# Feed-forward weights split at higher priority, the set-up moved behind a gate evacuation, the first weights in four pieces

## The chip, the cores and the metric
The kernel runs on one core of one Trainium2 chip. The metric is the device time of the whole program in microseconds (us); lower is better. A core has five engines with a queue each that runs in order: TensorE (PE, matmuls; its weight loads are PEld), VectorE (DVE), ScalarE (ACT), GpSimd (POOL) and SyncE (SP, which here only issues DMAs).

## What is computed
Two layers of a first block, each of them a gated feed-forward, an attention mixer and a second feed-forward, then two layers of a second block, each of them a hybrid attention and a feed-forward. There are 256 tokens of width 1024, all in fp32. The six feed-forward stages are what the change touches:

```python
def swiglu(x, w_gate, w_up, w_down):
    return (jax.nn.silu(x @ w_gate) * (x @ w_up)) @ w_down
# first block, per layer (D_FF = 2816):
x = x + 0.5 * swiglu(rms_norm(x, norm_ffn1[l]), w_ffn1_gate[l], w_ffn1_up[l], w_ffn1_down[l])
x = x + hybrid_mixer(rms_norm(x, norm_mix[l]), ...)
x = x + 0.5 * swiglu(rms_norm(x, norm_ffn2[l]), w_ffn2_gate[l], w_ffn2_up[l], w_ffn2_down[l])
# second block, per layer:
gate, up = jnp.split(h @ w_ffn_in, 2, axis=-1)
return x + (jax.nn.silu(gate) * up) @ w_ffn_out
```

## The kernel before
fp32 products are made of parts: each operand is split into a high part hi and a low part lo, and the product is the sum of hi by hi, hi by lo and lo by hi. `weights` (L177) loads a tile of weights, 1 MB, from HBM into a buffer named raw (three of them; the DMA is issued on SP, L174) and splits it in two halves: ACT copies to hi (L188), DVE subtracts to lo (L189). Of hi and lo there are four buffers each; one comes free when the matmuls that read it are done.

A feed-forward stage (`ffn`, L289) goes over the 22 blocks of 128 hidden columns in chunks of four (the last chunk, number 5, has two). Of a chunk it makes first the gate product, then the up product. A product is two tiles of weights (half 0 and half 1, 512 rows of the width each, `product`); for each block and each of four k it runs one matmul of 512 columns with hi (L310) and one of 256 columns with lo (L314). The four blocks of a gate product go into the four PSUM banks named acc, those of an up product into psS, psT, psS and psO. Each bank is then evacuated (`total`): ACT copies one half (low, L322), DVE adds the other (g or u, L324). The gate is multiplied on POOL by the row factor rbc (L339), goes through tanh on ACT (L341), a DVE step (L342) and one more POOL multiply (L349); with u, POOL makes hh (L351), and that is split by ACT (gh, L222) and DVE (gl, L223). The down product (`to_residual`, L251 to L256) follows, with eleven tiles of weights.

In the first stage `start` (L1397) puts the beginning together: transposes of x's first column half on PE (`piece`, L1453) with their split on ACT (L1462) and DVE (L1463), the first tile of weights tied behind the last of these by `behind`, which orders instructions of the same engine only, and then the loads of x's second half (`load_x`, on SP), its squares and pieces. The constants that later stages need are set up by `extra` (L1384): `more_consts` makes two transposes (L137, L140) into acc banks and copies from them on DVE (gcol, L138, and others), `angles` makes one more transpose (L936) into an acc bank and tables of sine and cosine. It is called after chunk 2 of the first stage.

Each engine's order is worked out ahead by a list planner over the whole program: of the instructions that its own clock has as ready on an engine (inputs made, a buffer free) it takes the one with the lowest place, and the place is the instruction's number in the program. Inside `high_priority(p)` the numbers are p lower. So instructions of a later stage can run early, and the order on the chip is then fixed: an instruction at the head of a queue that isn't ready holds up all behind it.

Of the kernel before, what the change touches and what calls it, by code (L numbers as in the profile page):

```python
# [33 lines left out]
class K:  # L34
# [142 lines left out]
    def weights(self, src, shape, pieces=1):  # L177

        nc = self.nc
        with self.tc.high_priority(self.ahead) if self.ahead else nullcontext():  # L180
            raw = self.wraw(src, shape, pieces)
            hi = self.wp.tile([128] + shape, F32R, tag="hi", name="hi", bufs=4)
            lo = self.wp.tile([128] + shape, F32R, tag="lo", name="lo", bufs=4)
            n = shape[0] // 2
            for h in range(2):
                hs = slice(h * n, (h + 1) * n)
                self.last_w = (
                    nc.scalar.activation(hi[:, hs], raw[:, hs], AF.Copy),  # L188
                    nc.vector.tensor_tensor(lo[:, hs], raw[:, hs], hi[:, hs].bitcast(F32), op=ALU.subtract),  # L189
                )  # L190
                if h == 0:
                    self.first_w = self.last_w
        return hi, lo
# [37 lines left out]
    def to_residual(self, yh, yl, w, nk, scale, after, held=2, fill=False):  # L231
# [49 lines left out]
        if fill:  # L281
            return [(None, lambda c=c: fetch(c), lambda hl, c=c: run(c, hl), None) for c in range(nch)], end
        for c in range(nch):
            for _ in run(c, fetch(c)):
                pass
# [3 lines left out]
    def ffn(self, pr, wg, wu, wd, scale, after, start=None, load=None, extra=None):  # L289
        nc, tc = self.nc, self.tc  # L290
        xx = pr.xx
        self.n_ft = -1
        with tc.tile_pool(name="ffn", bufs=2) as fp:
            gh = fp.tile([128, NF, S], F32R, name="gh", bufs=1)
            gl = fp.tile([128, NF, S], F32R, name="gl", bufs=1)

            def product(w, c, n, banks, first):

                cs = slice(c * 512, c * 512 + n * 128)
                for h in range(2):  # L300
                    src = w[h * 512 : (h + 1) * 512, cs].rearrange("(k p) f -> p k f", p=128)
                    if first and h == 0:
                        hi, lo = start(lambda: self.weights(src, [4, n * 128], 2))
                    else:
                        hi, lo = self.weights(src, [4, n * 128])
                    for j in range(n):
                        fs = slice(j * 128, (j + 1) * 128)
                        for k in range(4):
                            xk = xx[:, 4 * h + k]
                            nc.tensor.matmul(  # L310
                                banks[j], hi[:, k, fs], xk.rearrange("p u s -> p (u s)"),
                                start=h == 0 and k == 0, stop=False,
                            )
                            self.last = nc.tensor.matmul(  # L314
                                banks[j][:, 0:S], lo[:, k, fs], xk[:, 0, :],
                                start=False, stop=h == 1 and k == 3,
                            )

            def total(bank, name):

                low = fp.tile([128, S], F32, tag="low", name="low")
                nc.scalar.copy(low, bank[:, S : 2 * S])  # L322
                v = fp.tile([128, S], F32, tag=name, name=name, bufs=5)
                nc.vector.tensor_tensor(v, bank[:, 0:S], low, op=ALU.add)  # L324
                return v

            for c in range((NF + 3) // 4):
                n = min(4, NF - 4 * c)
                banks = [self.acc() for j in range(n)]
                product(wg, c, n, banks, start is not None and c == 0)  # L330
                if c == 0:
                    pr.finish()
                    if load is not None:
                        load()
                    pr.broadcast()
                sgs = []
                for j in range(n):
                    g = total(banks[j], "g")
                    nc.gpsimd.tensor_tensor(g, g, pr.rbc, op=ALU.mult)  # L339
                    th = fp.tile([128, S], F32, name="th")  # L340
                    nc.scalar.activation(th, g, AF.Tanh, scale=0.5)  # L341
                    nc.vector.scalar_tensor_tensor(g, th, 1.0, g, op0=ALU.add, op1=ALU.mult)  # L342
                    sgs.append(g)
                banks = [self.ft() for j in range(n)]
                product(wu, c, n, banks, False)
                for j in range(n):
                    f = 4 * c + j
                    u = total(banks[j], "u")
                    nc.gpsimd.tensor_tensor(sgs[j], sgs[j], pr.rbc, op=ALU.mult)  # L349
                    hh = fp.tile([128, S], F32, name="hh")  # L350
                    nc.gpsimd.tensor_tensor(hh, sgs[j], u, op=ALU.mult)  # L351
                    self.split(gh[:, f, :], gl[:, f, :], hh)
                if extra is not None and c == 2:
                    with tc.high_priority(150):
                        extra()
            self.to_residual(
                lambda k: gh[:, k, :], lambda k: gl[:, k, :], wd, NF, 0.5 * scale, after
            )


    def proj_item(self, name, w, c0, n, pr, done):


        def fetch():
            return [
                self.weights(
                    w[h * 512 : (h + 1) * 512, c0 : c0 + n].rearrange("(k p) f -> p k f", p=128), [4, n]
                )
                for h in range(2)
            ]  # L370

        def run(hl):
            ps = [self.acc() for t in range(2)]
            for h in range(2):
                for t in range(2):
                    ts_ = slice(t * 128, (t + 1) * 128)
                    for j in range(4):
                        k = 4 * h + j
                        self.mm3(
                            ps[t][:, 0:n], pr.xh[:, k, ts_], pr.xl[:, k, ts_], hl[h][0][:, j, :], hl[h][1][:, j, :],  # L380
                            start=k == 0, stop=k == KT - 1,
                        )
                        yield 3 * (n / 2400 + 0.013)
            done(ps)

        return name, fetch, run, None
# [972 lines left out]
    def run(self):  # L1359
# [19 lines left out]
        def prep(i):  # L1379
            gi, l, _ = st[i]  # L1380
            fin = gi == 3 and l == 0 and i > 0
            return Prep(self, self.gfin if fin else self.gcol[:, gi, l, :], fin)

        def extra():  # L1384
            with self.behind((self.last, *self.last_w)):
                self.more_consts()
                self.angles()
# [9 lines left out]
        def start(weights):  # L1397

            for t in range(2):
                pr.piece(t, 0, self.ft, False)  # L1400
            with self.behind(self.last_p):
                hl = weights()
            with self.behind(self.first_w):
                self.load_x(1)
                for t in range(2):
                    pr.square(t, 0)
                    pr.piece(t, 1, self.ft)
            return hl
# [4 lines left out]
                for t in range(2):  # L1413
                    pr.piece(t, n, self.ft)
        for i, (gi, l, fn) in enumerate(st):
            self.ahead = 0
            if i + 1 < len(st):
                box = []

                def after(t, n, i=i, box=box):  # L1420
                    if not box:
                        box.append(prep(i + 1))
                    box[0].piece(t, n)
            else:
                def after(t, n):
                    ns = slice(n * 512, (n + 1) * 512)
                    nc.sync.dma_start(self.out[0, t * 128 : (t + 1) * 128, ns], self.x[:, t, ns])

            by_token = i + 1 < len(st) and st[i + 1][0] in (1, 3)
            after.order = [(u, v) if by_token else (v, u) for u in range(2) for v in range(2)]  # L1430
            fn(pr, after, **({"start": start, "load": self.loads, "extra": extra} if i == self.first == 0 else {}))
            once.close()
            if i + 1 < len(st):
                pr = box[0]
# [172 lines left out]
```

## Time and profile before
| what | value |
|---|---|
| median of 3 runs | 1923.4 us (1920.32 to 1925.4) |
| the profiled execution | 1922.36 us |
| its span, from first to last instruction | 1920.7 us |
| PE busy | 1824.2 us (95%) |
| DVE busy | 1312.5 us (68%) |
| ACT busy | 1000.1 us (52%) |
| POOL busy | 618.9 us (32%) |
| read from HBM | 311.61 MB |

The profile is of one execution. A row of a timeline gives the start and the length in us, the engine, the line of the kernel, the operation, what it writes and reads, how many it merges, and in brackets how long its engine was idle before it and which instruction or transfer ended that. A share of busy time is a mean over stages with different limits, so the rows are read stage by stage.

### The profile page before, as it was taken

The numbers are of one execution on the slowest core, as the hardware profiler recorded it, in microseconds if no ns is written. First come the engines' busy times: TensorE is split into PE (matmuls) and PEld (weight loads), VectorE is DVE, ScalarE is ACT, GpSimd is POOL, SyncE is SP. The second block draws the span as 40 slices with busy tenths as digits, with TensorE's granted clock in tenths as the row PEclk, the third lists the DMA queues.
The fourth block names the chain that finished last, engine by engine and source line by source line (L and its number), as shares of the span: only waits on it lengthen the run. The fifth ranks groups of instructions, "written<-read, shape, count | busy, mean of one in ns | idle before, by whom it ended". The sixth has DMA issues, their size and how long they took to land.

```text
span 1920.7 us, 27216 instructions
## 1 busy us (share of the span) xinstructions
PE 1824.2 (95%) x10136; PEld 1521.3 (79%) x10136; DVE 1312.5 (68%) x2170; ACT 1000.1 (52%) x1948; POOL 618.9 (32%) x660
## 2 busy tenths in 40 slices
PE   8899989999999999899999987899999897999999
PEld 7788866788788878667887776798888786888887
DVE  6766567776677665677766587767765787667763
ACT  6554445655555454456555544545554544546552
POOL 6451112254225411112542254012441442014540
PEclk9999999999999999999999998999999998999999
DMA  7547462354655464623546534245546444255543
GB/s 241 193 134 242 158 192 91 112 186 146 239 173 186 144 241 147 206 88 112 183 147 232 177 110 153 89 153 176 181 149 228 151 132 153 89 176 175 170 168 123
DMA packets 149077, 314.42 MB, mean 164 GB/s; under 512 B 5588, under 2 KB 30320, under 8 KB 148944
## 3 DMA queue, kind: packets, MB, share of 16 engines
q1 hardware_dynamic: 148016, 311.15, 49.4%
q0 software_dynamic: 896, 1.52, 0.4%
q8 instruction: 80, 1.31, 0.3%
q14 instruction: 53, 0.43, 0.1%
q10 hardware_dynamic: 32, 0.01, 0.0%
HBM read 311.61 MB, written 1.05 MB: 163 GB/s over the span
## 4 chain that ended last, share of the span: by engine, by line
PE 62%; DVE 17%; POOL 9%; ACT 7%; issue 4%; DMA 1%; SPq 0%; ACTq 0%; POOLq 0%; DVEq 0%
DVE lo L189 9%; PE acc L310 8%; PE acc L252 8%; PE acc L251 8%; PE acc L256 8%; PE acc L314 4%; PE acc L209 3%; PE psS L310 3%; ACT hi L188 3%; PE acc L210 3%; PE acc L211 3%; POOL hh L351 2%; POOL g L339 2%; ACT P L441 2%; PE psT L310 2%
## 5 line engine op out<-in xcount | busy, mean ns | idle before, releaser
L189 DVE TENSOR_TENSOR lo<-raw,hi 128x1024 fp32r<-128x1024 f32 (+1 forms) x604 | 745.3, 1258 | 206.7 <-ACT hi L188 202.3
L188 ACT ACTIVATE hi<-raw 128x1024 fp32r<-128x1024 f32 (+1 forms) x604 | 590.3, 1009 | 197.2 <-PE acc L256 110.8
L310 PE MATMUL acc<-xx,hi 128*128 128x512 f32 x1056 | 371.8, 397 | 8.0 <-DVE gcol L138 7.4
L314 PE MATMUL acc<-xx,lo 128*128 128x256 f32 x1056 | 291.4, 279 | 0.0
L310 PEld LDWEIGHTS acc<-xx,hi 128*128 128x128 f32 x1056 | 198.6, 189 | 53.0 <-DVE gcol L138 7.7
L252 PE MATMUL acc<-lo,gh 128*128 128x512 f32 x528 | 209.9, 397 | 3.8 <-DVE lo L189 3.8
L251 PE MATMUL acc<-hi,gh 128*128 128x512 f32 x528 | 209.4, 397 | 0.0
L314 PEld LDWEIGHTS acc<-xx,lo 128*128 128x128 f32 x1056 | 199.7, 189 | 1.8
L339 POOL TENSOR_TENSOR g<-g,rbc 128x256 f32<-128x256 f32 x132 | 136.4, 1046 | 175.1 <-DVE g L324 121.3
L310 PE MATMUL psS<-xx,hi 128*128 128x512 f32 x528 | 190.7, 395 | 2.1 <-ACT hi L188 2.1
L351 POOL TENSOR_TENSOR hh<-g,u 128x256 f32<-128x256 f32 x132 | 139.6, 1065 | 162.2 <-DVE u L324 162.2
L256 PE MATMUL acc<-hi,gl 128*128 128x512 f32 x528 | 173.7, 395 | 0.0
L209 PE MATMUL acc<-hi,xx 128*128 128x512 f32 (+2 forms) x416 | 171.2, 412 | 0.2 <-ACT xx L1462 0.2
L211 PE MATMUL acc<-hi,xx 128*128 128x512 f32 (+2 forms) x416 | 161.8, 389 | 1.1 <-DVE xx L1463 1.0
L210 PE MATMUL acc<-lo,xx 128*128 128x512 f32 (+2 forms) x416 | 161.5, 389 | 0.0
L349 POOL TENSOR_TENSOR g<-g,rbc 128x256 f32<-128x256 f32 x132 | 134.8, 1027 | 65.4 <-DVE g L342 65.4
L222 ACT ACTIVATE gh<-hh 128x256 fp32r<-128x256 f32 x132 | 55.2, 418 | 180.8 <-POOL hh L351 180.3
L314 PE MATMUL psS<-xx,lo 128*128 128x256 f32 x528 | 147.3, 279 | 1.1 <-DVE lo L189 1.1
L341 ACT ACTIVATE th<-g 128x256 f32<-128x256 f32 x132 | 55.0, 417 | 153.0 <-POOL g L339 152.6
L342 DVE SCALAR_TENSOR_TENSOR g<-th,g 128x256 f32<-128x256 f32 x132 | 83.4, 635 | 73.2 <-ACT th L341 73.2
L252 PEld LDWEIGHTS acc<-lo,gh 128*128 128x128 f32 x528 | 99.1, 188 | 28.6 <-DVE lo L189 5.4
L223 DVE TENSOR_TENSOR gl<-hh,gh 128x256 fp32r<-128x256 f32 x132 | 57.7, 437 | 92.2 <-ACT gh L222 92.2
(429 smaller groups left out, 3486.9 us busy)
## 6 DMA issues: line engine op xcount, KB each, us to landing
raw<-in_w_in_dram SPq DMA_DIRECT2D x60, 1024.0 KB, 5.1
raw<-in_w_ffn_down_dram SPq DMA_DIRECT2D x44, 1024.0 KB, 5.0
raw<-in_w_ffn_up_dram SPq DMA_DIRECT2D x40, 1024.0 KB, 5.1
raw<-in_w_ffn_in_dram SPq DMA_DIRECT2D x40, 1024.0 KB, 5.2
raw<-in_w_ffn_gate_dram SPq DMA_DIRECT2D x39, 1024.0 KB, 5.1
raw<-in_w_ffn_out_dram SPq DMA_DIRECT2D x22, 1024.0 KB, 5.0
raw<-in_w_out_dram SPq DMA_DIRECT2D x12, 1024.0 KB, 4.9
raw<-in_w_ffn_gate_dram SPq DMA_DIRECT2D x10, 512.0 KB, 3.8
```

What stands on the lines that cost most here:

```text
L188: nc.scalar.activation(hi[:, hs], raw[:, hs], AF.Copy),
L189: nc.vector.tensor_tensor(lo[:, hs], raw[:, hs], hi[:, hs].bitcast(F32), op=ALU.subtract),
L209: mm(out, ah, bh, start=start, stop=False)
L210: mm(out, ah, bl, start=False, stop=False)
L211: self.last = mm(out, al, bh, start=False, stop=stop)
L251: mm(accs[t, n], ah, hi[:, j, cs], start=k == 0, stop=False)
L252: mm(accs[t, n], ah, lo[:, j, cs], start=False, stop=False)
L256: mm(accs[t, n], al, hi[:, j, cs], start=False, stop=k == nk - 1)
L310: nc.tensor.matmul(banks[j], hi[:, k, fs], xk.rearrange("p u s -> p (u s)"), start=h == 0 and k == 0, stop=False,)
L314: self.last = nc.tensor.matmul(banks[j][:, 0:S], lo[:, k, fs], xk[:, 0, :], start=False, stop=h == 1 and k == 3,)
L339: nc.gpsimd.tensor_tensor(g, g, pr.rbc, op=ALU.mult)
L351: nc.gpsimd.tensor_tensor(hh, sgs[j], u, op=ALU.mult)
```

## The change
In the six feed-forward stages (stage kinds 0, 2 and 4) `weights` now runs at priority 200; before, `ahead` was 0 for all stages. That covers the DMA of each tile of feed-forward weights, its splits, and the buffers that they take. `extra` is called between the evacuation of chunk 2's gate product and its up product, at no raised priority; before, it was called after the evacuation of that chunk's up product at priority 150. The first tile of weights is loaded and split in four pieces of 128 x 512; before, in two of 128 x 1024.

```diff
@@ weights
-            n = shape[0] // 2
-            for h in range(2):
+            n = shape[0] // max(2, pieces)
+            for h in range(max(2, pieces)):
                 hs = slice(h * n, (h + 1) * n)
@@ ffn, product
                     if first and h == 0:
-                        hi, lo = start(lambda: self.weights(src, [4, n * 128], 2))
+                        hi, lo = start(lambda: self.weights(src, [4, n * 128], 4))
@@ ffn, chunk loop
                     sgs.append(g)
+                if extra is not None and c == 2:
+                    extra()
                 banks = [self.ft() for j in range(n)]
                 product(wu, c, n, banks, False)
...
                     self.split(gh[:, f, :], gl[:, f, :], hh)
-                if extra is not None and c == 2:
-                    with tc.high_priority(150):
-                        extra()
@@ run
         for i, (gi, l, fn) in enumerate(st):
-            self.ahead = 0
+            self.ahead = 200 if gi in (0, 2, 4) else 0
```

## Rows read from the trace of the kernel before

**Rows 1.** PE's timeline, then DVE's, first stage, 82 to 92 us.
```profile
82.76 0.50 PE L310 MATMUL acc<-xx,hi 128*128 128x512 f32 x1 [0.58 <-DVE g L324]
...
91.80 0.80 PE L310 MATMUL acc<-xx,hi 128*128 128x512 f32 x1 [7.38 <-DVE gcol L138]
...
90.86 0.41 DVE L324 TENSOR_TENSOR u<-psS,low 128x256 f32<-128x256 f32 x1
...
91.53 0.21 DVE L138 COPY gcol<-acc 128x64 f32<-128x64 f32 x1
```

**Rows 2.** Stretches: length; busy of PE, PEld, DVE, ACT, POOL; PEclk, DMA, GB/s.
```profile
91.80:94.60 2.80, 2.80 (x9) 2.41 (x10) 2.80 (x14) 1.89 (x4) 0.48 (x2) 0.50 0.53 205
95.00:105.00 10.00, 10.00 (x60) 8.74 (x59) 7.17 (x18) 7.70 (x13) 4.57 (x4) 1.00 0.42 118
```

**Rows 3.** Waits of PE over the whole run: us in total, times, longest.
```profile
PE acc L252 <- DVE lo L189: 3.8, 5, 0.8
...
PE psS L310 <- ACT hi L188: 2.1, 4, 0.6
...
PE psS L314 <- DVE lo L189: 1.1, 5, 0.2
```

**Rows 4.** Timelines of PE, then DVE, second feed-forward stage, chunks 2 and 3.
```profile
419.78 0.28 PE L314 MATMUL acc<-xx,lo 128*128 128x256 f32 x1
...
441.96 0.28 PE L314 MATMUL acc<-xx,lo 128*128 128x256 f32 x1
...
421.09 0.75 DVE L324 TENSOR_TENSOR g<-acc,low 128x256 f32<-128x256 f32 x2
...
423.23 0.41 DVE L324 TENSOR_TENSOR g<-acc,low 128x256 f32<-128x256 f32 x1
...
426.89 0.41 DVE L324 TENSOR_TENSOR g<-acc,low 128x256 f32<-128x256 f32 x1
...
444.11 0.75 DVE L324 TENSOR_TENSOR g<-acc,low 128x256 f32<-128x256 f32 x2
```

**Rows 5.** Timelines of ACT, DVE, then PE, second stage's last chunk.
```profile
481.28 0.42 ACT L222 ACTIVATE gh<-hh 128x256 fp32r<-128x256 f32 x1 [1.45 <-POOL hh L351]
...
484.42 0.63 ACT L188 ACTIVATE hi<-raw 128x512 fp32r<-128x512 f32 x1
...
482.52 0.69 DVE L189 TENSOR_TENSOR lo<-raw,hi 128x512 fp32r<-128x512 f32 x1
...
483.68 0.39 PE L310 MATMUL psS<-xx,hi 128*128 128x512 f32 x1
...
485.10 0.51 PE L310 MATMUL psS<-xx,hi 128*128 128x512 f32 x1 [0.56 <-ACT hi L188]
```

**Rows 6.** POOL's timeline, second stage, chunk 2.
```profile
423.38 0.75 POOL L349 TENSOR_TENSOR g<-g,rbc 128x256 f32<-128x256 f32 x1 [0.36 <-DVE g L342]
...
424.96 1.72 POOL L349 TENSOR_TENSOR g<-g,rbc 128x256 f32<-128x256 f32 x1
```

**Rows 7.** The start: timelines of PE, ACT, DVE, SP, then a DMA's landing.
```profile
3.88 1.11 PE L1453 MATMUL psS<-ident,x 128*128 128x128 f32 x4
4.78 1.06 PE L1453 MATMUL psT<-ident,x 128*128 128x128 f32 x4
...
12.60 2.06 PE L310 MATMUL acc<-xx,hi 128*128 128x512 f32 x4
...
25.51 0.60 PE L1500 MATMUL psO<-ident,nr 128*128 128x128 f32 x4
...
4.04 1.28 ACT L1462 ACT_TABLE_LOAD   x1 [4.04 <-DVE gcol L87]
...
8.64 0.35 DVE L1463 SCALAR_TENSOR_TENSOR xx<-psT,gcol,xx 128x128 fp32r<-128x128 f32 x1 [0.17 <-ACT xx L1462]
...
4.36 8.10 SPq L174 DMA_DIRECT2D raw<-in_w_ffn_up_dram  x2
...
raw<-in_w_ffn_up_dram SPq DMA_DIRECT2D x1, 1024.0 KB, 12.9
```

## The prediction
> **What bounds the kernel now.** Three views were read in this order: TensorE's (PE's) waits, its timeline where it waits, then the queues of ScalarE (ACT), VectorE (DVE) and GpSimd (POOL) there. Inside the feed-forward stages PE hardly ever stops: a gate or up product of a four-tile chunk, 32 pairs of matmuls, takes 11.1 us, and the gate products of chunks 2 and 3 of the second stage end 22.18 us apart, two products with nothing between [rows 4]. So only PE's idle time can be won, and what the change touches are three kinds of it.
>
> First, the gap in the first stage. The next gate product waits 0.58 us for a bank, runs four pairs and then waits 7.38 us for the copy of gcol [rows 1]. That copy's own transpose had run before 82.8 us; the copy ran only at 91.53, because DVE takes its queue in order and the copy stood behind the up evacuation of the third bank, at 90.86 [rows 1]. When PE resumed, its granted clock was 0.50, the lower of its two levels (1.2 GHz), for 2.8 us: 9 matmuls there, where 10 us at 1.00 hold 60 [rows 2]. So some 1.4 us more are lost. The gap costs 0.6 + 7.4 + 1.4 = 9.4 us.
>
> Second, late splits: PE's waits for hi or lo of weights add up to 2.1 + 1.1 + 3.8 = 7.0 us [rows 3], in five stages of six, at the short last chunk. In the second stage the up product waits at 485.10 for a hi that ACT ran at 484.42, behind evacuations [rows 5].
>
> Third, the start: steady products begin at 12.60 us [rows 7], after x has landed, has been transposed and split.
>
> The evacuation chain (ACT copy, DVE add, POOL multiply, ACT tanh and so on) is nearly as slow as PE: from one chunk to the next its first add moves from 421.09 to 444.11, 23.02 us, where PE needs 22.18 [rows 4]. It falls 0.84 us further behind with every chunk. This backlog is what put the gcol copy and the splits late.
>
> **Part 1, splits at priority 200.** A chunk is some 195 instructions, so a split now stands before its whole chunk's evacuation wherever both are ready in the order that the planner works out. Work on the engines is the same; no instruction is added except in the first tile. In the last chunk the two splits of the second up half, the later of which ran at 484.42, move to directly behind the evacuation step at 481.28 [rows 5]. From 481.7, two hi pieces of 0.63 us and a lo of 0.69 behind the second end at 483.7, and PE is there at 483.7 [rows 5]: the wait there goes. The first down tile moves up with them, against a wait of 0.76 us (3.8 us in five waits) [rows 3]. I leave 1.4 of the 7.0 us for the stage whose backlog is longest: gain 5.6, between 7.0 (all) and below nothing (rival A). What is late next is the evacuation behind these splits; its banks are needed a whole product later (11.1 us) and the last banks come 7.2 us late (426.89 + 0.41 against 420.06) [rows 4], so 4 us cover it.
>
> At the five later stage starts the first splits now go before the halves of x that PE waits for. One split is some 1.3 us of ACT (two of 0.63) [rows 5]; PE has other products to run there. I take 0.5 us in all, between 0 and 5 (one split per stage).
>
> The raw loads in SyncE's (SP's) queue move too, and this is the costly part: SP issues all weights and x. Gate half 0, gate half 1 and up half 0 fit in the three raw buffers, so all three are ready at once; 200 places earlier they all stand before x's four loads. Before, x and these three tiles, 4 MB, ended with up half 0, which landed at 4.36 + 12.9 = 17.3 us [rows 7]. The same 4 MB now end with x. Between x's second 256 KB (in by 4.8) and 17.3 us 3.5 MB came, 0.9 us per 256 KB, so x's first halves are in at 17.3 - 1.8 = 15.5. From there to the last split of x's first halves took 4.2 us (4.78 to 8.64 + 0.35), of which 1.28 was a table load that is now over by then [rows 7]: 18.4. The first weight tile's split is tied behind that: 0.63 + 0.69 gives the first pair at 19.7, and three more pieces at 0.69 make the fourth pair 21.8. Twelve pairs at 0.35 and some 1 us of slow clock (a pair at 0.50 takes 0.62) [rows 2] end half 0 at 27.0, half 1 5.55 later at 32.5. Before, that product ended at 25.5 [rows 7]: loss 7.0. Bounds: 3.7 if up's tile comes after x (1 MB less, 3.5 us), 11 if the splits of the other two tiles (four more of some 1 us) are queued before x's second halves; and 0 is a rival.
>
> **Part 2, set-up after the gate evacuation of chunk 2.** Its three transposes follow that gate product's last matmul on PE, each into a bank that the same product has just filled. They used to follow the up product, 11.1 us later, with these banks long free. In the second stage the third bank is free 3.6 us after the product's end (423.23 + 0.41 - 420.06) [rows 4]. PE takes its queue in order: if the planner puts the three right there, the whole up product waits 3.6 us behind them. With 1.4 us of slow clock as before, 5.0 us. The old gap goes, since gcol's bank is then asked for a whole product later: gain 9.4 - 5.0 = 4.4. Bounds: 9.4 (transposes placed later, no wait) and 0.8 (the third bank as late as the fourth, 7.2). The set-up's copies on DVE, like that of gcol at 0.21 us [rows 1], and its ACT steps are as many as before; without priority 150 they fall behind the evacuation, and the 11.1 us of the up product hide them.
>
> **Part 3, four pieces.** One more pair of loads and two more splits of half the size: the first lo could be ready 0.6 us sooner, which PE sees only if nothing else is late; that is in the sum of part 1. PE's transposes of x's first two 256 KB loads start 0.9 us apart (3.88, 4.78) [rows 7], which is their transfer at the rate above, so two more loads cost nothing but 0.9 us of issue, under 10 us of transfers. The Trainium skill (DMA: Bandwidth & Descriptors, sections Anatomy of one DMA and Bandwidth) speaks against it: its rule is to batch to 1 MiB or more, and its fit has about 2 us fixed in each DMA, which would make four pieces an estimated 4 us dearer than two, and the time 1925; the 0.9 us in the trace does not bear that out for queued loads.
>
> **Sum.** +7.0 (start) - 4.4 (set-up) - 5.6 (late splits) + 0.5 (stage starts) = -2.5 us. The profiled execution took 1922.4 us (span 1920.7 and 1.7 around it), so 1919.9; the median of the runs shown is 1.0 above that execution: 1921.
>
> **Rivals.**
> A, slower: the backlog grows. Earlier splits put two lo subtractions (some 1.4 us each, two of 0.69) [rows 5] together in front of adds and multiplies of the evacuation. A POOL multiply takes 0.75 us alone and 1.72 beside such a split [rows 6]. If the backlog grew by 0.7 us more per chunk, the evacuation at 481.28 would come 2.8 us later by chunk 4, and the last splits, still behind it, would be 2.8 - 1.4 = 1.4 us later than now in five stages: the 5.6 gained go and 7 more are lost, 1921 + 12.6 = 1934. It decides from 0.35 us per chunk on. For it: the backlog exists. Against: the same splits run either way, and a multiply that comes behind both runs alone. Chance 0.13. The Trainium skill (SBUF — State Buffer, section Who interferes with whom) calls DVE's and GpSimd's shared port an exclusive lock whose loser fully blocks; these rows agree.
> B, x isn't late: SP keeps x first, or x is slipped in before the big tiles. Then 7.0 doesn't come: 1914. Against: nothing but the places orders loads that are all ready. Chance 0.15.
> C, the transposes stand later in PE's queue and find their banks free: 5 us better, 1916. For: their banks must be free in the planner's own account first. Chance 0.15.
> D, the change doesn't do what it says at the last chunk, because the splits there were not outranked but not ready: 1921 + 5.6 = 1927. Against: ACT ran copies and waited for POOL 1.45 us between them [rows 5]. Chance 0.12.
> The forecast as summed: 0.45, with 1915 to 1927 as its own range.
>
> **How the numbers follow.** A measurement of this kernel can tell 0.3%, 5.8 us, from no change: faster is under 1917.6, slower over 1929.2. Of the forecast case 0.09 is faster and 0.03 slower; of B 0.12 faster; of C 0.08 faster; of A 0.10 slower, of D 0.03 slower. Faster 0.29, slower 0.16, same 0.55. The range from 1911 to 1932 holds B with 3 us to spare and most of D, and leaves out the upper half of A and the lower ends of B.
>
> **What would show it.** Right: x's transposes on PE at about 15 us instead of 3.9 and the first gate product's end near 32; three transposes before the up product of chunk 2 with a wait of 3 to 5 us for g; no wait for gcol; PE's waits for hi and lo near 1 us in total. Wrong: x landing at 4 us (B); no wait at the transposes (C); waits for hi and lo at the last chunks as now (D) or longer (A).

## The result and the profile after

The changed kernel takes 1973.5 us, median of 4 runs (1970.8 to 1976.0), against 1921.9 for the kernel before (1919.0 to 1925.4): a ratio of 1.027, 95% interval 1.024 to 1.029. It is slower by 52 us, where 1921 had been forecast with a range up to 1932. The profiled execution has a span of 1969.9 us against 1920.7, so 49.2 us have to be found.

Cutting both traces at the starts of the gate/up work, of the down work and at its end gives the first table (us; stage 0 is the first of the six feed-forward stages).

| stretch | before | after | difference |
|---|---|---|---|
| up to the first gate matmul | 12.6 | 19.0 | +6.4 |
| gate/up of stage 0 | 134.7 | 133.4 | -1.3 |
| gate/up of stages 1 to 5 | 623.3 | 635.3 | +12.1 |
| down of stages 0 to 5 | 383.2 | 413.9 | +30.7 |
| everything else | 766.9 | 768.3 | +1.4 |

PE's waits of the changed kernel over the whole run name the places (us in total, times, longest; compare [rows 3]).

```profile
PE acc L251 <- DVE g L324: 13.6, 3, 5.1
PE acc L251 <- ACT hi L188: 10.6, 3, 4.3
...
PE psS L1452 <- DMA x<-in_x_dram: 10.2, 1, 10.2
PE acc L310 <- DVE xx L1462: 8.2, 8, 1.5
...
PE acc L137 <- DVE g L324: 4.4, 1, 4.4
...
PE acc L310 <- ACT hi L188: 1.6, 1, 1.6
...
PE acc L935 <- DVE g L324: 1.3, 1, 1.3
...
PE acc L252 <- DVE lo L189: 0.2, 1, 0.2
...
PE psS L314 <- DVE lo L189: 0.2, 1, 0.2
```

The late splits are cured: the three lines of [rows 3], 7.0 us, are down to 2.0, of which 1.6 is one new wait at the start. New are six waits at the starts of the down products (24.2 us, first two lines), the wait for x (10.2, before 4.8) and eight waits for xx at four stage starts (8.2).

**The down start.** PE's timeline of the changed kernel, stage 3: the last matmul of gate chunk 5, then the down product (start, duration).

```profile
1042.26 0.28 PE L314 MATMUL acc<-xx,lo 128*128 128x256 f32 x1
...
1048.03 0.39 PE L251 MATMUL acc<-hi,gh 128*128 128x512 f32 x1
...
1051.06 0.40 PE L252 MATMUL acc<-lo,gh 128*128 128x512 f32 x1
1055.72 0.47 PE L251 MATMUL acc<-hi,gh 128*128 128x512 f32 x1 [4.27 <-ACT hi L188]
```

DVE's timeline of the same stretch:

```profile
1045.82 2.58 DVE L189 TENSOR_TENSOR lo<-raw,hi 128x1024 fp32r<-128x1024 f32 x2 [0.46 <-ACT hi L188]
1048.33 0.41 DVE L223 TENSOR_TENSOR gl<-hh,gh 128x256 fp32r<-128x256 f32 x1
1048.66 0.41 DVE L324 TENSOR_TENSOR g<-acc,low 128x256 f32<-128x256 f32 x1
1049.00 2.89 DVE L189 TENSOR_TENSOR lo<-raw,hi 128x1024 fp32r<-128x1024 f32 x2
1051.81 0.41 DVE L342 SCALAR_TENSOR_TENSOR g<-th,g 128x256 f32<-128x256 f32 x1
1052.51 2.73 DVE L189 TENSOR_TENSOR lo<-raw,hi 128x1024 fp32r<-128x1024 f32 x2 [0.28 <-ACT hi L188]
1055.16 0.41 DVE L324 TENSOR_TENSOR g<-acc,low 128x256 f32<-128x256 f32 x1
```

Gate chunk 5 has only two blocks and filled two of the four accumulation banks by 1042.5. The down product's first row half takes the other two; its second half, 2.8 us later, takes these. The first comes free at 1049.07, in time; the second at 1055.16 + 0.41 = 1055.57, and PE goes on at 1055.72. Between the two adds stand four raised splits of down weights, 2.89 + 2.73 us. That the profile names "ACT hi" as releaser in three of the six cases is the last semaphore, not the cause: the second half multiplies the weights that the first half had already used.

The kernel before, DVE at the same place (three lines), then PE:

```profile
1018.71 0.42 DVE L324 TENSOR_TENSOR g<-acc,low 128x256 f32<-128x256 f32 x1
1019.04 1.21 DVE L189 TENSOR_TENSOR lo<-raw,hi 128x1024 fp32r<-128x1024 f32 x1
1020.17 0.41 DVE L324 TENSOR_TENSOR g<-acc,low 128x256 f32<-128x256 f32 x1
```

```profile
1020.84 0.39 PE L251 MATMUL acc<-hi,gh 128*128 128x512 f32 x1
```

There one split stood between the adds, the second bank was free at 1020.58, and PE wanted it at 1020.84. The cover was 0.26 us, and as little in the other four later stages; in the first it was 1.7.

The wait has two halves. Counted from the first matmul of up chunk 5 (1009.54 before, 1042.38 after), the second bank comes free after 11.04 us before and 13.19 after, 2.2 us later; and PE asks for it after 11.30 us before and 9.07 after, 2.2 us sooner, since the late splits no longer hold it up.

Each of these waits costs more than itself. The changed kernel's windows in the wait of stage 3, behind it, and later (length; busy of PE, PEld, DVE, ACT, POOL; PEclk, DMA share, GB/s):

```profile
1051.45:1055.72 4.27, 0.00 (x1) 0.03 (x1) 3.98 (x6) 4.13 (x6) 0.79 (x2) 1.00 0.90 316
1055.72:1060.00 4.28, 4.28 (x12) 3.37 (x13) 4.28 (x6) 1.09 (x3) 2.78 (x3) 0.61 0.81 285
1060.00:1064.00 4.00, 4.00 (x18) 3.20 (x18) 1.92 (x4) 2.31 (x3) 1.14 (x2) 0.99 0.83 271
```

After the idle stretch the granted clock is 0.61 over the next 4.3 us: most of them at the lower level, 1.2 GHz. 12 matmuls run there, where the next 4 us hold 18: 4.28 x 18 / 4.00 - 12 = 7 matmuls, some 1.6 us. With the 0.77 us of the old wait for lo gone, 4.27 + 1.6 - 0.77 = 5.1, against 4.9 measured for that stage's down stretch.

**The start.** PE's timeline of the changed kernel, then SP's queue (compare [rows 7]):

```profile
13.66 1.12 PE L1452 MATMUL psS<-ident,x 128*128 128x128 f32 x4 [10.17 <-DMA x<-in_x_dram]
...
18.96 2.07 PE L310 MATMUL acc<-xx,hi 128*128 128x512 f32 x4 [1.62 <-ACT hi L188]
```

```profile
0.80 2.29 SPq L174 DMA_DIRECT2D raw<-in_w_ffn_gate_dram  x5
3.13 0.51 SPq L174 DMA_DIRECT2D raw<-in_w_ffn_up_dram  x1
3.68 2.56 SPq L92 DMA_DIRECT2D x<-in_x_dram  x4
```

Six weight loads go out before x, as forecast, and the first gate matmul comes 6.4 us later.

**The set-up.** PE's timeline of the changed kernel behind gate chunk 2 of stage 0 (compare [rows 1]):

```profile
82.03 0.36 PE L137 MATMUL acc<-ident,rows 64*128 64x64 f32 x1 [4.42 <-DVE g L324]
82.37 0.44 PE L140 MATMUL acc<-ident,rows 106*128 106x106 f32 x1
84.13 0.26 PE L935 MATMUL acc<-ident,pf 2*128 2x2 f32 x1 [1.33 <-DVE g L324]
```

The wait for gcol is gone and 5.75 us of waits for the gate's banks stand in its place.

**A stage start.** PE at the start of stage 1, changed kernel: two waits that the kernel before doesn't have.

```profile
373.96 0.50 PE L310 MATMUL acc<-xx,hi 128*128 128x512 f32 x1 [0.57 <-DVE xx L1462]
...
377.45 0.50 PE L310 MATMUL acc<-xx,hi 128*128 128x512 f32 x1 [1.46 <-DVE xx L1462]
```

DVE, changed kernel, shows what xx stands behind, the raised pair of splits:

```profile
374.52 2.36 DVE L189 TENSOR_TENSOR lo<-raw,hi 128x1024 fp32r<-128x1024 f32 x2
376.80 0.60 DVE L1462 SCALAR_TENSOR_TENSOR xx<-psS,gcol,xx 128x128 fp32r<-128x128 f32 x2
```

**A second rhythm.** One difference has no wait at all. A gate product of 32 pairs in mid-stage, the kernel before, then the changed one (windows, columns as above):

```profile
430.99:442.08 11.09, 11.09 (x66) 9.70 (x65) 7.97 (x13) 6.68 (x13) 4.16 (x5) 1.00 0.60 192
```

```profile
444.94:456.24 11.30, 11.30 (x66) 9.81 (x65) 7.96 (x13) 6.58 (x13) 3.02 (x4) 1.00 0.57 179
```

The same matmuls at the same clock of 1.00 take 11.09 us in one and 11.30 in the other: 347 ns against 353 per pair, steadily, through all products from chunk 1 on in stages 1 to 5. Eight long and two short products make 8 x 0.21 + 2 x 0.10 = 1.9 us per stage, 9.4 in five. With the chunk-0 gate products slower by about 2 us in four stages (their waits for xx) and the last up products quicker by 1.25 us in four (the late splits), that is 9.4 + 7.7 - 5.0 = 12.1, the table's.

### The profile page after: what moved, and what is told of

Same layout as the page of the kernel before. It is cut to its first block, busy times and chain, and to the rows that moved or that the text cites. A ratio compares the mean times of both kernels' runs of the same rounds, so it can differ in the third digit from the quotient of the medians.

```text
span 1969.9 us, 27224 instructions
## 1 busy us (share of the span) xinstructions
PE 1842.6 (94%) x10136; PEld 1531.3 (78%) x10136; DVE 1313.0 (67%) x2172; ACT 996.5 (51%) x1950; POOL 554.8 (28%) x660
## 4 chain that ended last, share of the span: by engine, by line
PE 56%; DVE 21%; ACT 10%; POOL 7%; issue 5%; DMA 1%; SPq 0%; ACTq 0%; POOLq 0%; DVEq 0%
DVE lo L189 13%; PE acc L251 7%; PE acc L256 7%; PE acc L310 7%; PE acc L252 7%; ACT hi L188 5%; PE acc L314 3%; PE acc L209 3%; PE acc L211 3%; PE acc L210 3%; PE psS L310 3%; ACT P L440 2%; POOL g L339 2%; POOL hh L353 2%; PE psS L314 1%
## 5 line engine op out<-in xcount | busy, mean ns | idle before, releaser
L189 DVE TENSOR_TENSOR lo<-raw,hi 128x1024 fp32r<-128x1024 f32 (+2 forms) x606 | 748.5, 1270 | 244.4 <-ACT hi L188 240.8
L188 ACT ACTIVATE hi<-raw 128x1024 fp32r<-128x1024 f32 (+2 forms) x606 | 580.5, 1004 | 230.3 <-PE acc L256 149.7
L310 PE MATMUL acc<-xx,hi 128*128 128x512 f32 x1056 | 377.6, 401 | 9.8 <-DVE xx L1462 8.2
L251 PE MATMUL acc<-hi,gh 128*128 128x512 f32 x528 | 213.9, 405 | 24.2 <-DVE g L324 13.6
L339 POOL TENSOR_TENSOR g<-g,rbc 128x256 f32<-128x256 f32 x132 | 121.1, 928 | 180.1 <-DVE g L324 126.4
L353 POOL TENSOR_TENSOR hh<-g,u 128x256 f32<-128x256 f32 x132 | 107.7, 823 | 182.7 <-DVE u L324 181.2
L351 POOL TENSOR_TENSOR g<-g,rbc 128x256 f32<-128x256 f32 x132 | 119.2, 905 | 97.6 <-DVE g L342 97.6
L251 PEld LDWEIGHTS acc<-hi,gh 128*128 128x128 f32 x528 | 101.8, 193 | 51.2 <-ACT hi L188 26.6
L342 DVE SCALAR_TENSOR_TENSOR g<-th,g 128x256 f32<-128x256 f32 x132 | 69.3, 528 | 79.8 <-ACT th L341 79.8
L256 PEld LDWEIGHTS acc<-hi,gl 128*128 128x128 f32 x528 | 101.6, 192 | 24.5
```

The source lines that it names most:

```text
L251: mm(accs[t, n], ah, hi[:, j, cs], start=k == 0, stop=False)
L256: mm(accs[t, n], al, hi[:, j, cs], start=False, stop=k == nk - 1)
L310: nc.tensor.matmul(banks[j], hi[:, k, fs], xk.rearrange("p u s -> p (u s)"), start=h == 0 and k == 0, stop=False,)
```

## The experiments

Ratios are against runs of the kernel before on the same chip, with 95% intervals. Differences in us from the changed kernel compare medians of different chips, on which the kernel before had medians of 1921.9 to 1924.7 us.

**Priority alone.** The kernel before with the first line of the diff only.

```diff
-            self.ahead = 0
+            self.ahead = 200 if gi in (0, 2, 4) else 0
```

> The kernel before with priority 200 on the feed-forward weights as the only change (set-up where it was, first tile in two pieces). Theory: the priority alone makes the loss of 51.7 us; the changed kernel's trace puts +6.4 us at the start, +30.7 at the six down products, +12 in the gate and up products of the five later stages. So about 1972 us. Rival: the moved set-up takes a share, since its transposes now wait 5.8 us on PE; then this run is 4 us or more faster than the changed kernel, 1968 or less.

Measured: 1975.5 us, 1.026 (1.024 to 1.029). The whole loss is the priority's.

**Everything but the priority.** The changed kernel with that line undone.

```diff
-            self.ahead = 200 if gi in (0, 2, 4) else 0
+            self.ahead = 0
```

> The changed kernel without the priority: set-up after chunk 2's gate evacuation and four first pieces remain. Theory: the old gap of 9.4 us is replaced by a wait of the transposes for their banks of 3 to 9 us, so 1917 to 1922 us against 1921.9 of before, and no later stage differs from before. Rival: the set-up itself upsets the later stages, then well over 1925.

Measured: 1924.0 us, 0.9994 (0.9985 to 1.0003), where the kernel before takes 1924.7 on this chip. The move of the set-up and the four pieces together are worth nothing. PE's waits of this kernel show why: the gap for gcol has turned into one as long for the gate's first bank.

```profile
PE acc L137 <- DVE g L324: 7.9, 1, 7.9
...
PE acc L935 <- DVE g L324: 1.3, 1, 1.3
```

**Down weights not raised.** The changed kernel, with this in `fetch`:

```diff
-            return self.weights(src, [2, D])
+            ahead, self.ahead = self.ahead, 0
+            hl = self.weights(src, [2, D])
+            self.ahead = ahead
+            return hl
```

> The changed kernel with the down products' weights back at their own places; gate and up weights stay raised. Theory: the splits of down's first tiles, now ahead of the last chunk's gate evacuation, hold two acc banks that down's second half needs; without that PE's wait of 4.2 to 5.1 us in five stages (2.1 in the first) and the slow clock behind it go, some 30 us: about 1943. Rival: PE waits there for the splits themselves (three of the six waits are put down to hi); then nothing is gained, or it becomes worse: 1973 or more.

Measured: 1940.8 us, 1.008 (1.007 to 1.010): 32.8 us less than the changed kernel. The waits at the down starts are gone from its trace. Waits for hi and lo outside the start stay at 1.1 us in all, so raising the gate and up splits, chunk 0's among them, cures the late splits without the down weights.

**Last gate banks first.** Undoing the raise also moves transfers, so this run keeps all weights raised and moves the suspected adds instead, with the ACT copies in front of them.

```diff
                 for j in range(n):
-                    g = total(banks[j], "g")
+                    with tc.high_priority(400) if c == 5 else nullcontext():
+                        g = total(banks[j], "g")
```

> The changed kernel, all weights raised as there, and the evacuation (copy and add) of gate chunk 5, the short one, raised above the down weights' splits. Theory (down product waits because its banks for the second row half are those of gate chunk 5, whose adds stand behind the raised splits on DVE): the 4 us waits at the six down starts go though the down weights stay raised; about 1943 to 1948, near the run with the down weights not raised. Rival (the down starts suffer from the raised down weights' transfers or from their hi and lo, not from the adds' place): 1965 or more.

Measured: 1938.9 us, 1.010 (1.007 to 1.013). Its DVE timeline at the same place, stage 3:

```profile
1034.23 0.41 DVE L324 TENSOR_TENSOR g<-acc,low 128x256 f32<-128x256 f32 x1
1034.57 0.41 DVE L223 TENSOR_TENSOR gl<-hh,gh 128x256 fp32r<-128x256 f32 x1
1034.90 1.76 DVE L189 TENSOR_TENSOR lo<-raw,hi 128x1024 fp32r<-128x1024 f32 x1
1036.58 0.41 DVE L324 TENSOR_TENSOR g<-acc,low 128x256 f32<-128x256 f32 x1
1036.92 4.03 DVE L189 TENSOR_TENSOR lo<-raw,hi 128x1024 fp32r<-128x1024 f32 x3
```

The second add follows 2.35 us after the first, not 6.5, with the raised splits behind it, and of the waits at the down starts (PE's waits) 1.0 us is left of 24.2; the six down stretches together take 380.0 us, in the changed kernel 413.9:

```profile
PE acc L251 <- DVE g L324: 1.0, 2, 0.5
```

So it is the adds' place in DVE's queue, and neither the transfers nor hi and lo.

**x first.** The changed kernel with x's loads ahead of all weights.

```diff
-            self.nc.sync.dma_start(self.x[:, t, ns], self.a["x"][0, t * 128 : (t + 1) * 128, ns])
+            with self.tc.high_priority(1000):
+                self.nc.sync.dma_start(self.x[:, t, ns], self.a["x"][0, t * 128 : (t + 1) * 128, ns])
```

> The changed kernel with x's four loads ahead of all others. Theory: the first gate product ends 6.3 us sooner, as in the kernel before, and nothing else changes: 1967. Rival: the late start gave the splits time to run ahead and later waits grow by as much: 1971 to 1974.

Measured: 1968.1 us, 1.023 (1.021 to 1.026): 5.4 us less. The rival held in part. The first gate matmul comes at 9.5 us, but up product 0 now waits 2.7 us for hi and lo and gate product 0 2.1 us for xx, and the first down product starts at 151.1 us, only 1.3 before that of the changed kernel. So this run doesn't price the start by itself.

**Chunk 0 not raised.** The changed kernel, in `product`, with `stage_ahead` set where `ahead` was:

```diff
                 cs = slice(c * 512, c * 512 + n * 128)
+                self.ahead = self.stage_ahead if c else 0
```

> The changed kernel, but the weights of each stage's chunk 0 keep their own place; chunks 1 to 5 and the down weights stay raised. Theory (three separate causes: the first chunk's weights ahead of x and of the xx operations at each stage start; the down weights ahead of the last gate chunk's evacuation; the slower matmul rhythm): x comes first again (the 6.4 us at the start go), the waits of the first product for xx go (8.2 us over 8 waits), the waits at the six down starts (4 us each) stay: about 1959. If the rhythm of 353 ns per pair is set at the stage start it goes back to 347 in stages 1 to 5, 2 us a stage more: about 1949. Rival (the rhythm comes with raised weights of the later chunks): 353 stays, about 1959. If the stage starts were not a cause of their own: 1968 or more.

Measured: 1956.5 us, 1.017 (1.016 to 1.019), 17.0 less than the changed kernel. The start is 10.4 us, no wait for xx is left at a feed-forward stage start, and stages 1 to 5 run at 347 ns per pair again. The gain lies between the two expectations because the waits at the down starts grew: in five stages to 5.1 us each (before this edit 4.2 to 5.1), and the six down stretches from 413.9 to 421.7 us. In four of the five stages the second add now ends 8.85 us after the down product's start, where it ended after 7.5.

**Only gate and up of chunks 1 to 5.** The last edit and that of the down weights together, so both down weights and chunk 0 stand at their own places.

> Only gate and up weights of chunks 1 to 5 are raised; chunk 0 and the down weights keep their own places; set-up place and the four pieces as in the changed kernel. Theory (raising hurts only where it overtakes the evacuation before the down product and the xx operations at a stage start): no wait at a down start, none for xx, the waits for hi and lo at the last chunk (5.6 us in all) gone, set-up gap about 6.5 us against 8 before: about 1916 to 1919 with the rhythm at 347 ns. Rival (the raised weights of the middle chunks cost by themselves, by the backlog or the rhythm): 1930 or more.

Measured: 1918.8 us, 0.9976 (0.9967 to 0.9986). All the loss is gone and a little is gained, so raised splits in mid-stage cost nothing. But the late splits are not cured here, against the expectation: PE's listed waits for hi and lo fall from 7.0 to 2.9 us, yet in stage 1 the last up product takes 6.79 us to the first down matmul (480.93 to 487.72), 6.95 in the kernel before and 5.65 in the changed one, and the other later stages are alike. Why the last chunk's splits run late again when chunk 0 keeps its own place is open. The set-up still waits 5.08 + 1.33 = 6.41 us for the gate's banks.

**Two pieces.** That kernel with the first weights in two pieces.

```diff
-                        hi, lo = start(lambda: self.weights(src, [4, n * 128], 4))
+                        hi, lo = start(lambda: self.weights(src, [4, n * 128], 2))
```

> The run with only chunks 1 to 5 of gate and up raised, with the first weights in two pieces as before. Theory of the prediction (the pieces cost and give nothing on the path): within 2 us of that run, 1917 to 1921, start of the first product the same within 0.5 us. Rival (smaller pieces bring the first matmul forward): the start later by up to 1 us. The rhythm of stage 0, 353 ns in that run before the set-up and 347 after it, would go to 347 throughout if the four pieces are what draws it, about 1 us.

Measured: 1918.0 us, 0.9973 (0.9964 to 0.9983): the same. The first gate matmul comes at 10.9 us, with four pieces at 11.1. Stage 0 stays at 353 ns, so the pieces don't set the rhythm. With two pieces up product 0 waits 4.28 us for a lo, and the set-up's waits are 1.7 us where they were 6.4: what PE loses at the one place it has back at the other.

**The set-up in another bank.** The kernel with gate and up of chunks 1 to 5 raised, and `rows` and `rows2` transposed into one bank of tag O behind gate product 3:

```diff
                 product(wg, c, n, banks, start is not None and c == 0)
+                if extra is not None and c == 3:
+                    extra()
...
-        pc = self.acc()
+        pc = self.psO()
         nc.tensor.transpose(pc[:, 0:64], self.rows, self.ident[0:64, 0:64])
...
-        pc = self.acc()
-        nc.tensor.transpose(pc[:, 0:106], rows2, self.ident[0:106, 0:106])
+        nc.tensor.transpose(pc[:, 64:170], rows2, self.ident[0:106, 0:106])
...
```

> As the run with only chunks 1 to 5 of gate and up raised, and the constants' two transposes go into one bank of tag O, behind gate product 3 and ahead of its evacuation, where that bank has been free for long; no accumulation bank is asked for. Theory (the set-up's PE gap is a wait for a bank that an evacuation must free, not the work of the set-up): the gap of about 6.5 us falls below 1.5 us, so 5 us less than that run: about 1912. Rival (the set-up's gap comes back elsewhere, at up product 3 that needs bank O again 8.5 us later): no gain, within 2 us of that run.

Measured: 1920.1 us, 0.9986 (0.9977 to 0.9996). No gain; three waits of 0.53, 4.65 and 1.37 us (6.55) are as long as the two before them, 6.41. The longest is the third transpose, of pf, which still asked for an accumulation bank. So that one went into bank O as well, all three ahead of the reads.

> As the run with the two constants' transposes in bank O behind gate product 3, with the third one (pf, which there still asked for an accumulation bank and waited 4.65 us) in the same bank, all three ahead of the copies that read it. Theory: no accumulation bank is asked for any more, the set-up's PE gaps, 6.5 us there, fall below 1.5 us: 1914 to 1915. Rival (the set-up's DVE work, some 5 us, pushes back the evacuation of gate chunk 3 and up product 3 or gate product 4 wait instead): 1918 or more.

Measured: 1921.3 us, 0.9991 (0.9980 to 1.0002). The rival held: the transposes wait 1.77 us for bank O, and up product 3 waits 4.74, in all 6.51 us. PE's timeline of this kernel:

```profile
104.54 0.77 PE L318 MATMUL psO<-xx,hi 128*128 128x512 f32 x1 [4.74 <-DVE pos L941]
```

Now up product 3 waits for the last of the bank's reads, which stood behind two splits. The next kernel takes the bank out with one copy:

```diff
+        cols = self.op.tile([128, 172], F32, name="cols")
+        nc.vector.tensor_copy(cols, pc[:, 0:172])
+        pc = cols
...
```

> As the run with all three transposes in bank O, but one DVE copy of 172 columns takes them out of the bank and the set-up reads that copy. There up product 3 waited 4.74 us for the last of seven reads of the bank, which stood behind two splits; the bank's only read now ends near 101.1 us and the product wants it at 99.8. Theory: set-up gaps of 1.8 + 1.3 = 3.1 us against 6.5: 1915 to 1917. Rival (the gap is the lag of DVE and comes back at whatever DVE must free next, as it did twice): 1918 or more.

Measured: 1914.7 us, 0.9958 (0.9946 to 0.9970). This is the lowest median of all, and below both kernels. The transposes wait 1.61 us, up product 3 2.93 (PE's timeline below): 4.54, 1.9 less than before the three edits. Gate/up of stage 0 went from 134.7 to 132.6. The other 2 us are not shown to be this edit's: outside the feed-forward stages and the start its profiled execution takes 763.2 us and that of the kernel with gate and up raised 768.2, but that of the kernel with two pieces, whose set-up is the old one, takes 762.6.

```profile
101.55 0.51 PE L321 MATMUL psO<-xx,hi 128*128 128x512 f32 x1 [2.93 <-DVE cols L143]
```

**Extra transposes.** What sets the rhythm? The changed kernel, with one extra transpose ahead of four up products in stage 0, two in stage 1, up to six in stage 5.

```diff
+                if 1 <= c <= 4:
+                    for d in range(self.dummies):
+                        nc.tensor.transpose(banks[0][:, 0:128], self.ident, self.ident)
                 product(wu, c, n, banks, False)
...
```

> The changed kernel with 1 to 6 extra 128x128 transposes of the identity (one in the first feed-forward stage, six in the last) ahead of the up products of chunks 1 to 4, into the bank that this product then starts afresh; 84 transposes in all, at some 0.1 us each about 8 us more work. Theory (the rhythm of 347 or 353 ns per pair is redrawn by any interruption of the matmul sequence and then kept): behind the extra transposes some products run at 347 and others at 353 within stages 1 to 5, up products changing with the count; total between 1970 and 1982. Rival (the rhythm belongs to what runs beside it in the stage, the raised splits and their transfers, or to where the weights lie): 353 throughout stages 1 to 5 as in the changed kernel, about 1981.

Measured: 1971.8 us, 1.026 (1.024 to 1.027). Windows over the gate products of chunks 1, 2, 4 and 5 in stage 1 (that of chunk 3 is like chunk 2's):

```profile
399.56:410.86 11.30, 11.30 (x66) 9.79 (x65) 7.95 (x13) 6.40 (x12) 3.03 (x4) 1.00 0.57 186
422.19:433.28 11.09, 11.09 (x66) 9.78 (x65) 7.74 (x13) 6.34 (x14) 3.03 (x4) 1.00 0.56 176
...
467.23:478.53 11.30, 11.30 (x66) 9.79 (x65) 7.86 (x14) 6.56 (x14) 3.77 (x5) 1.00 0.32 88
489.86:495.41 5.55, 5.55 (x35) 4.89 (x34) 2.82 (x6) 1.72 (x6) 2.00 (x3) 1.00 0.73 247
```

The first runs as in the changed kernel, chunk 2 as in the kernel before, chunk 4 as in the changed kernel again; 5.55 us for chunk 5's 16 pairs is the shorter rhythm. Each product takes one of two lengths. Beside it runs the same raised work. The theory held: the rhythm is a state of the matmul sequence that can change when something breaks in. The 84 extra transposes cost nothing on balance.

## Why the prediction was wrong

**The step that failed** stands in part 1: "What is late next is the evacuation behind these splits; its banks are needed a whole product later (11.1 us) ... so 4 us cover it." For a chunk of four blocks this holds; no wait for a bank appears there. At the last chunk the up product has 16 pairs, 5.65 us, and down's second row half asks for gate chunk 5's banks 2.8 us after that. The trace of before had the answer, 0.26 us of spare time where 4 us had been assumed; the rows were read from chunk 2 and used for all chunks. And four raised splits (5.6 us of DVE) went in front of an add with that cover, while the cured late splits, the prediction's own gain, brought PE there 2.2 us sooner. This step alone is 30.7 of 49.2 us; the run with the adds raised shows it, 34.7 us back.

**Mis-sized: the other stage starts.** Taken at 0.5 us, between 0 and 5. In four stages the chunk-0 gate product grew by some 2 us each, 7.7 in all, above the upper bound: the bound counted one split per stage, and DVE ran a pair of 2.36 us in front of xx.

**Not foreseen: the rhythm**, 9.4 us in five stages. Nothing in the trace of before showed that a product could take 11.30 us at full clock.

**Right: the start.** Forecast +7.0, measured +6.4; x's transposes at 13.66 rather than about 15. The named sign, the first gate product's end near 32, isn't there: its last matmul starts at 36.28, as 25 matmuls of up product 0 run between its own. But gate product 1, behind both, starts at 43.53 against 37.05 before, 6.5 us later, and with chunk 0 not raised at 34.59: the loss is that of chunk 0's raised weights. Rival B (x isn't late) falls.

**Right: the late splits.** Forecast -5.6; of 7.0 us of waits 0.4 are left, beside the 1.6 at the start. Rival D falls for this kernel; where chunk 0 isn't raised, the last up products stay late.

**Mis-sized: the set-up.** Forecast -4.4; the stretch that holds it gained 1.3, or some 2.3 without the slower rhythm of five products in it (0.21 us each). The third bank was taken as free 3.6 us after the gate product's end, from the second stage (stage 1). In the first DVE lags further: the first bank came at 82.0, 4.4 us after the product's end at 77.6, the third at 84.1, 6.5 after it. Without the priority the whole trade is worth nothing. Rival C (no wait) falls.

**Right in the total: four pieces at nothing.** 1918.0 with two and 1918.8 with four, within the intervals; that the extra wait of the run with two pieces at up product 0 and its shorter waits at the set-up cancel was not forecast. The loads themselves cost little more: up half 0, behind them in the queue, landed at 16.0 us with two pieces and 16.4 with four. The 0.9 us between x's transposes, which the prediction read as the loads', are PE's own pace: the second four ran behind the first without a gap [rows 7], and in the changed kernel all four sets come 0.85 to 0.91 us apart. The Trainium skill (DMA: Bandwidth & Descriptors, section Anatomy of one DMA) has some 2 us fixed in each DMA, a fit to DMAs that GpSimd issues; taken over to these loads, which SP issues, it would have made four pieces an estimated 4 us dearer. The run doesn't bear that out for loads queued one behind another.

**Rival A named the right side and the wrong mechanism.** Its backlog should have grown by over 0.35 us more per chunk. Gate adds and products of stage 1, chunks 2 and 3, in the changed kernel (compare [rows 4]), DVE then PE:

```profile
434.61 0.74 DVE L324 TENSOR_TENSOR g<-acc,low 128x256 f32<-128x256 f32 x2
...
457.93 0.75 DVE L324 TENSOR_TENSOR g<-acc,low 128x256 f32<-128x256 f32 x2
```

```profile
433.52 0.28 PE L314 MATMUL acc<-xx,lo 128*128 128x256 f32 x1
...
456.12 0.28 PE L314 MATMUL acc<-xx,lo 128*128 128x256 f32 x1
```

The first add moves by 23.32 us while PE takes 22.60: 0.72 per chunk, before 0.84. The backlog grew more slowly. What had grown was not the chain but the distance between two of its steps at one place.

Nearly every sign that the prediction named as "right" appeared: x late, a wait of 3 to 5 us for g (4.4, and 1.3 more), none for gcol, waits for hi and lo at 2.0 us. They covered the steps that had been thought of, and the loss lay where none was looked for.

## What to carry to other kernels

Raising work puts something else behind it: list every place where an operation of that class now overtakes, and read the spare time at each from its own rows, the short last chunk and the stage ends above all; a full chunk's cover says nothing about them. Raise only what is late, and leave at its place what nobody waits for; then look at the time of the product that was late, and not only at its listed waits. A wait for a bank that a late engine must free doesn't go away by choosing another bank; it shrinks when the late engine has less to do before it can free it.

## What the hardware showed

The same pairs of matmuls (512 and 256 columns), at a granted clock of 1.00, run steadily at 347 or at 353 ns per pair, 2% apart. A change of rhythm was seen only where the sequence was broken, by a wait or by a few other matmuls, and a rhythm lasts at least until the next break: over a whole stage of 100 us in most kernels here, over one or two products in the one with extra transposes. The run with chunk 0 not raised had 347 in stages 1 to 5 and the changed kernel 353. The run with the last adds raised had the waits for xx in stage 5 too and yet ran at 347 there, so these waits don't decide it alone. The run with the set-up taken out by one copy had 353 in stage 2, though it had chunk 0 at its own place as well. What decides between the two is open.
